# A decoder block: the third group's attention keys computed by seven products in the stage of the queries

## The chip, the cores and the metric

The kernel runs on one core of one Trainium2 chip. The time is the device time of one execution in microseconds; smaller is better. Five engines work beside each other, each with an instruction queue of its own that it takes in order: PE (TensorE, matrix products; PEld is its weight load), DVE (VectorE), ACT (ScalarE), POOL (GpSimd) and SP (SyncE, which here only starts transfers). Transfers (DMA) are issued from the queues of SP, POOL or ACT and run on 16 engines of their own. [...]

## The reference

For one sequence of 1024 tokens and width 1024, the block computes `h`, a normalized and modulated input, then one projection `h @ w_in` that is cut into parts, and from these a retention branch, an attention branch and gates; a squared-ReLU MLP follows. What matters here is the attention:

```
ATT_GROUPS = ((128, 1), (512, 4), (2048, 16))     # window, dilation; 4 heads of 128 each
for gi, (win, dil) in enumerate(ATT_GROUPS):
    aq, ak, av = parts[4 + 3 * gi], parts[5 + 3 * gi], parts[6 + 3 * gi]
    ...
    s = einsum(q, k) * dh ** -0.5 + bias           # banded, in blocks of 128 queries
    mx = max(s); e = exp(s - mx); den = sum(e); p = e / den; lse = mx + log(den)
    o = einsum(p, v)
wts = softmax(stack(lses), axis=0)                 # over the three groups
att = einsum('gbhs,gbhsd->bshd', wts, outs)
merged = sigmoid(gate_a) * ret_out + sigmoid(gate_b) * att_out
```

All is in float32.

## The kernel before

*Precision.* A float32 factor is split into a high part (`hi`, a cast) and a low part (`lo`, what is left), and a product is three matmuls: low by high, high by low, high by high (`mm3`, lines 207, 209, 211). The cast is made by ACT, the subtraction by DVE. So whatever PE is to multiply needs one instruction on each of the two first.

*Two ways to project.* Plain: `proj_gen` takes a head's weights (128 columns) and goes through the 1024 inputs in 8 k-steps; a k-step is 6 matmuls of 128x128 by 128x512 (two halves of the tokens, three terms), so a head takes 48. By seven products: the class `Blocks` takes a pair of heads (256 columns) as a 2 x 2 block problem and makes seven block products instead of eight, with sums of blocks before and after on DVE; each product is 12 matmuls, so a pair takes 84 where the plain way takes 96. The stage `queries_keys` runs 18 such pairs, in the order of the string `"rargrargrargrargaa"`: r are the queries and keys of the retention (each followed by a rotation on DVE, spread over the next pair), a the attention queries, g eight of the gates. Loads of a pair are issued when the pair two ahead of it starts. `a_out` evicts the results; attention queries are stored to DRAM (`aq_d`) and read again in the attention stage.

*The order around the change.* After the queries come the values, then the retention by heads and chunks, and then the attention, for two pairs of heads one after the other. The whole is a list of steps (`Steps`). A step has a body and a list of loads; each load is 512 KB into one of three buffers (`raw`), and has a function that splits it for PE. A buffer is loaded again as soon as its split is done. The splits of the next step's loads are emitted at the start of a step (`following`), or, for steps marked "late" or True, where the body calls for them. Nothing is scheduled by a planner: the engines' queues have the order in which the body emits.

*The attention of one pair of heads* has six key steps (`att_step`), in the order group 1, 2, 0 and within it head 0, 1. Step i projects one head's keys (8 k-steps) and weaves between the k-steps the scores of the step before (`scores_gen`, a "bank" being one PSUM bank of score blocks: three banks for group 1, two for group 2, four for group 0; `lag=2` means that the first bank comes after three k-steps). At its end it splits the new keys from PSUM (`k_split`, lines 1488 and 1489) and calls `scores_end` on the woven scores: maximum on DVE (lines 1529 to 1539), then eight exponentials on ACT (line 1542). After the second head of groups 1 and 2, `stats_out` stores maxima and sums to DRAM and reads them back in token order, both from SP. Then come gate steps (`cover_step`), which project gates so that PE has work: step 0 weaves the last scores, and emits `scores_end`, `weights` (the mix over groups), `pscale` (scaling of group 0's probabilities, lines 1645 and 1647), and the copy of the raw gate out of PSUM (lines 1827, 1828); step 1 is the gate alone; step 2 starts the products of probabilities and values (`pv`, each with a transpose, a split and its matmuls). The second pair's first key step lies beside the last of these products.

*Other work that lies there.* At the first key step the last head of the retention is finished (`u_final`: scale on ACT, product on DVE, store of `y` from SP, lines 687 to 690). Afterwards the sums of `y` blocks that the retention's output product wants are made by POOL's accumulating transfers, two at each projection (`with_sums`, `result_sum`, lines 572 and 574), each waiting for the one before. The bias tiles are loaded by SP at the end of the first key step (`bias_load`, line 1466).

Of the kernel before, what the change touches and what calls it, by code (L numbers as in the profile page):

```python
# [11 lines left out]
F32 = mybir.dt.float32  # L12
# [5 lines left out]
P = 128  # L18
D = 1024
S = 1024  # L20
# [120 lines left out]
def block_kernel(ctx, tc, io, stop=None, dbg=None):  # L141
# [537 lines left out]

    def u_final(h, es=range(4)):  # L680
        for e in es:
            i = h * 4 + e
            t = hd["on", h][e]
            for hf in range(2):
                neg = 16 if hf == i % 2 else 0
                b = t[:, 512 * hf:512 * hf + 512]
                nc.scalar.activation(b, b, AF.Identity, scale=gnv[0][:, neg + i:neg + i + 1],
                                     bias=gnv[1][:, neg + i:neg + i + 1])
            nc.vector.tensor_mul(t, t, hd["srg", h, e])
            nc.sync.dma_start(y_d[h][:, 2 * (i % 2):2 * (i % 2) + 2, e // 2], t.rearrange("p (t x) -> p t x", t=2))  # L690

# [78 lines left out]
    va_d = [dram.tile([S, 512], F32, name=f"vad{g}") for g in range(3)]  # L770
    aq_d = {(p, g, a): dram.tile([P, S], F32, name=f"aqd{p}{g}{a}") for p in range(2) for g in range(3) for a in range(2)}
    h12_d = [dram.tile([P, 2, 512], F32, name=f"h12d{m}") for m in range(4)]
    xn, wa = [], []
# [361 lines left out]
    g_pairs = [("g", i) for i in range(len(GATES) // 2)]  # L1135
    PAIRS = [{"r": r_pairs, "a": a_pairs, "g": g_pairs}[i].pop(0) for i in "rargrargrargrargaa"]
    NA = len(PAIRS)
    OA = {}

    def a_load(q, part):  # L1140
        pair = PAIRS[q]
        src = io[{"g": "w_gate2", "a": "w_aq"}.get(pair[0]) or f"w_r{pair[1]}"]
# [22 lines left out]
    def a_out(q, n, x, y=None):  # L1165
# [5 lines left out]
        o, view = OA[q][i][:, 512 * t:512 * t + 512], lambda z: z  # L1171
        if pair[0] == "a" and pair[1] == 1:
            o = OA[q][i].rearrange("p (r n i) -> p r n i", r=4, n=2)[:, :, t, :]
            view = lambda z: z.rearrange("p (i r) -> p r i", r=4)
        elif pair[0] == "a" and pair[1] == 2:
            o = OA[q][i].rearrange("p (r i) -> p r i", r=8)[:, :, 64 * t:64 * t + 64]
            view = lambda z: z.rearrange("p (i r) -> p r i", r=8)
# [7 lines left out]
        if n in ("12", "21"):  # L1185
            if pair[0] == "g":
                dst = gate_d[GATES[2 * pair[1] + i]]
            elif pair[0] == "a":
                dst = aq_d[pair[2], pair[1], i]
            else:  # L1190
                return
            nc.sync.dma_start(dst, OA[q][i])
# [282 lines left out]
    def q_prep(pair, g, a):  # L1475
# [6 lines left out]
        return prep  # L1482

    def k_split(pair, g, a, ps):

        hi, lo = ring(f"kh{pair}{g}{a}"), ring(f"kl{pair}{g}{a}")
        src, h_, l_ = by_blocks(ps, g), shaped(hi, g), shaped(lo, g)
        nc.scalar.copy(h_, src)
        nc.vector.tensor_sub(l_, src, fv(h_))
        A["k", g, a] = (hi, lo)  # L1490
# [34 lines left out]

    def scores_end(pair, g, a):
        p, t, st = A["p"], A["P", g, a], A["st"]
# [10 lines left out]
        ng = p.tile([P, 8], F32, tag="ng", bufs=2, name=f"ng{pair}{g}{a}")  # L1538
        nc.vector.tensor_scalar_mul(ng, st[:, g, :, a], -1.0)  # L1539
        for blk in range(8):  # L1540
            v = pslice(g, t, blk)[0]
# [58 lines left out]
    def stats_out(pair, g):  # L1600

        if g == 1:
            A["stn"] = A["p"].tile([P, 3, 8, 4], F32, tag="stn", name=f"stn{pair}")
        d = dram.tile([S, 4], F32, name=f"std{pair}{g}")
        nc.sync.dma_start(natural(d, g, 4), blocks(A["st"][:, g], g))
        nc.sync.dma_start(A["stn"][:, g], natural(d, 0, 4))

# [142 lines left out]

    combos = [(g, a) for g in (1, 2, 0) for a in range(2)]

    def att_step(pair, i):

        g, a = combos[i]

        def body(*args):
            ps = ps_mm(f"ak{pair}{i}")
            gen = with_sums(proj_gen(ps, args[-1]))
            if i == len(combos) - 2:  # L1760
                v_fetch(pair, 0)
            if i > 0:
                last = combos[i - 1]
                weave(gen, NK, scores_gen(pair, *last), len(SB[last[0]]), lag=2)
            elif pair == 0:
# [4 lines left out]
                drain(gen)  # L1770
                u_final(H - 1)
                for h in range(H):
# [3 lines left out]
            else:  # L1776

                gen = at(at(gen, 3, args[0]), NK - 1, lambda: k_split(pair, g, a, ps))
                weave_pv(gen, NK - 1, 0, 2)
            if i == 0:  # L1780
                A["st"] = A["p"].tile([P, 3, 8, 4], F32, tag="st", name=f"st{pair}")
                bias_load(pair)
            if i > 0 or pair == 0:
                k_split(pair, g, a, ps)
            if i > 0:
                scores_end(pair, *last)
                if last[1] == 1:
                    stats_out(pair, last[0])
        return body

    def cover_step(pair, n):
# [4 lines left out]
        def body(*args):  # L1796
            ps = ps_mm(f"gate0{i}")
            gen = with_sums(proj_gen(ps, args[-1]))
            if n == 0:
                v_fetch(pair, 1)  # L1800
                weave(gen, 6, scores_gen(pair, *combos[-1]), len(SB[0]), lag=2, rest=False)
                drain(gen)
                v_split(pair, 0, False)
                scores_end(pair, *combos[-1])
                weights(pair)
# [12 lines left out]
            else:  # L1818
                gen = at(at(gen, 3, lambda: [pscale(2, a) for a in range(2)]), 4, lambda: args[0](1))
                gen = at(at(at(gen, 6, lambda: v_split(pair, 2)), 6, args[0]), 6, sigmoids)  # L1820
                weave_pv(gen, NK - 1, pair, 1)
            if n > 1:
                t = A["r1"].tile([P, S], F32, tag="att", bufs=8, name=f"g0{i}s")
# [19 lines left out]
    for pair in range(2):  # L1843
        for i, (g, a) in enumerate(combos):
            steps.add(att_step(pair, i),
                      [wsplit(io["w_ak"][g * 4 + 2 * pair + a])] +
                      ([(aq_d[pair, *combos[i - 1]], q_prep(pair, *combos[i - 1]))] if i > 0 else []),
                      manual=("late" if pair else True) if i == 0 else False)
        for n in range(len(COVER[pair])):
            more = [(aq_d[pair, *combos[-1]], q_prep(pair, *combos[-1]))] if n == 0 else []  # L1850
            steps.add(cover_step(pair, n), more + [wsplit(io["w_gate"][len(COVER[0]) * pair + n])], manual={2: True, 3: "late"}.get(n, False))

# [898 lines left out]
def pack(x, c, w_ada, b_ada, norm1_g, w_in, rel_bias, ret_gn_g, ret_gn_b,  # L2751
# [18 lines left out]
        "w_aq": _pairs(att[:, :, 0].reshape(1024, 1536)),  # L2770
        "w_ak": _cols(att[:, :, 1].reshape(1024, 1536)),
        "w_av": _vcols(att[:, 0, 2], 512),
# [29 lines left out]
```

## Time and profile before

Three runs took 2181.95 to 2182.26 us, median 2182.03.

| | |
|---|---|
| profiled execution | 2182.64 us, span 2180.9 us |
| PE busy | 2156.0 us (99%), 10084 matmuls |
| DVE busy | 1491.7 us (68%) |
| ACT busy | 942.8 us (43%) |
| POOL busy | 164.0 us (8%) |
| granted clock of PE | 0.999 |
| moved by DMA | 416.78 MB, mean 191 GB/s |

Times in rows are microseconds from the span's start, durations of single instructions in the groups are in ns. L is a line of the kernel. A row of the timeline gives start, duration, engine, line, operation, output <- inputs, shape, count, and in brackets how long the engine was idle before it and which instruction ended that. A row of the chain of waits gives who waited for whom, the total, the number of times and the longest. Rows that follow each other closely and are alike are merged (x2). Matmuls are pipelined: PE starts the next before the last has ended, so their durations add up to more than the time that they take.

### The profile page before, as it was taken

To read this page: it belongs to the slowest core of one execution; us is meant where nothing else is said; L and a number is where in the kernel's file an instruction comes from. 1 tells how busy PE (TensorE), PEld (TensorE's weight loads), DVE (VectorE), ACT (ScalarE), POOL (GpSimd) and SP (SyncE) were. 2 spreads that over 40 slices of the span, in tenths; PEclk is the share of its full clock that TensorE was granted. 3 is DMA by queue.
4 is the path that set the end of the run, shared out by engine and by line. 5 is a ranking of instruction groups with operands and counts; after the bars stand their busy time and mean duration, and the time that the engine had idled before them with its cause. 6 is when DMAs were issued, how large, how long until landed. Compare 5 with 4: busy or idle time off the path is not lost. (4 is left out here: it accounts for less than half of the span.)

```text
span 2180.9 us, 27323 instructions
## 1 busy us (share of the span) xinstructions
PE 2156.0 (99%) x10084; PEld 1791.6 (82%) x10084; DVE 1491.7 (68%) x2333; ACT 942.8 (43%) x1729; POOL 164.0 (8%) x195
## 2 busy tenths in 40 slices
PE   8999999999999999999999999999999999999998
PEld 6888888888878888888888888888778888888887
DVE  5985777774467877854655644776876665877855
ACT  5553323323434544544644625434454545533413
POOL 0001111100012212211100000001000000000003
PEclk9999999999999999999999999999999999999999
DMA  9859998844685555557763275654254435645322
GB/s 383 289 209 297 296 298 257 243 119 174 237 301 170 198 174 194 181 172 190 184 167 108 81 268 189 224 186 139 65 182 150 153 136 194 249 137 175 111 87 78
DMA packets 160881, 416.78 MB, mean 191 GB/s; under 512 B 27749, under 2 KB 55660, under 8 KB 157676
## 3 DMA queue, kind: packets, MB, share of 16 engines
q1 hardware_dynamic: 151416, 368.67, 47.9%
q0 software_dynamic: 9008, 46.14, 9.9%
q8 instruction: 79, 1.29, 0.2%
q14 instruction: 54, 0.44, 0.1%
q10 hardware_dynamic: 324, 0.23, 0.0%
HBM read 319.93 MB, written 156.13 MB: 218 GB/s over the span
## 5 line engine op out<-in xcount | busy, mean ns | idle before, releaser
L207 PE MATMUL qap<-hh,qaw 128*128 128x512 f32 x216 | 84.0, 389 | 0.0
L209 PE MATMUL qap<-hl,qaw 128*128 128x512 f32 x216 | 84.0, 389 | 0.0
L211 PE MATMUL qap<-hh,qaw 128*128 128x512 f32 x216 | 84.0, 389 | 0.0
L617 POOL TENSOR_TENSOR j<-qk,j 128x512 fp32r<-128x512 f32 x32 | 43.2, 1351 | 412.4 <-ACT j L616 393.8
L2122 POOL TENSOR_TENSOR accnf<-accnf,sqnf 128x256 f32<-128x256 f32 (+1 forms) x18 | 16.6, 922 | 609.9 <-ACT sqnf L2118 609.9
L2226 ACT ACTIVATE a<-a 128x512 f32<-128x512 f32 x48 | 30.3, 631 | 73.7 <-DVE a L2225 73.7
L1542 ACT ACTIVATE P<-P,ng 128x128 f32<-128x128 f32 (+1 forms) x96 | 42.0, 439 | 36.6 <-DVE ng L1539 36.6
L2434 ACT CAST w2h<-w2s 128x512 fp32r<-128x512 f32 x36 | 22.4, 622 | 78.7 <-DVE w2s L2472 78.7
L264 DVE TENSOR_TENSOR fw<-w1r,fw 128x512 fp32r<-128x512 f32 x48 | 32.9, 688 | 33.6 <-ACT fw L254 33.6
L1957 DVE TENSOR_TENSOR rwl<-rwl,rwh 128x1024 fp32r<-128x1024 f32 x25 | 30.2, 1220 | 29.1 <-ACT rwh L1987 29.1
L207 PE MATMUL fp<-h2h,fw 128*128 128x512 f32 x128 | 50.0, 391 | 0.0
L211 PE MATMUL fp<-h2h,fw 128*128 128x512 f32 x128 | 49.8, 389 | 0.0
L209 PE MATMUL fp<-h2l,fw 128*128 128x512 f32 x128 | 49.8, 389 | 0.0
L207 PE MATMUL roa<-rh,rwl 128*128 128x512 f32 x128 | 49.8, 389 | 0.0
L209 PE MATMUL roa<-rl,rwh 128*128 128x512 f32 x128 | 49.8, 389 | 0.0
L211 PE MATMUL roa<-rh,rwh 128*128 128x512 f32 x128 | 49.8, 389 | 0.0
L652 ACT COPY sm<-sT 128x128 f32<-128x128 f32 x32 | 8.5, 266 | 93.7 <-PE sT L640 93.7
L207 PEld LDWEIGHTS qap<-hh,qaw 128*128 128x128 f32 x216 | 40.5, 188 | 8.5
L209 PEld LDWEIGHTS qap<-hl,qaw 128*128 128x128 f32 x216 | 40.5, 188 | 8.4
L211 PEld LDWEIGHTS qap<-hh,qaw 128*128 128x128 f32 x216 | 40.5, 188 | 8.4
L2122 POOL TENSOR_TENSOR accn<-accn,sqn 128x512 f32<-128x512 f32 x12 | 15.5, 1293 | 386.1 <-ACT sqn L2118 386.1
L1947 ACT ACTIVATE rh<-rl 128x512 fp32r<-128x512 f32 x56 | 31.7, 623 | 23.4 <-PE roc L209 8.4
(3097 smaller groups left out, 7251.4 us busy)
## 6 DMA issues: line engine op xcount, KB each, us to landing
v<-vd SPq DMA_DIRECT2D x32, 512.0 KB, 4.5
raw<-in_w_ada_dram SPq DMA_DIRECT2D x32, 512.0 KB, 5.3
w1r<-in_w_ff_dram SPq DMA_DIRECT2D x32, 512.0 KB, 4.6
yt<-y POOLq DMA_DIRECT2D x24, 512.0 KB, 7.6
xsd<-as SPq DMA_DIRECT2D x24, 512.0 KB, 2.8
w2r<-in_w_ff2s_dram SPq DMA_DIRECT2D x24, 512.0 KB, 6.9
em<-in_w_ada_dram SPq DMA_DIRECT2D x16, 512.0 KB, 10.2
wrvs<-in_w_rv_dram POOLq DMA_DIRECT2D x16, 512.0 KB, 10.0
```

What stands on the lines that cost most here:

```text
L207: nc.tensor.matmul(o, wl, xh, start=first, stop=False, skip_group_check=skip)
L209: nc.tensor.matmul(o, wh, xl, start=False, stop=False, skip_group_check=skip)
L211: nc.tensor.matmul(o, wh, xh, start=False, stop=last, skip_group_check=skip)
L264: nc.vector.tensor_sub(t[:, 512:], src, fv(t[:, :512]))
L617: nc.gpsimd.tensor_sub(t[:, 1], src, fv(t[:, 0]))
L652: nc.scalar.copy(sm, ps[:, :C])
L1542: nc.scalar.activation(v, v, AF.Exp, bias=ng[:, blk:blk + 1], accum_out=st[:, g, blk, 2 + a:3 + a])
L1947: nc.scalar.activation(hi, fv(lo), AF.Copy, scale=sign)
L1957: nc.vector.tensor_sub(lo, fv(lo), fv(hi))
L2122: (nc.vector if f == 7 else nc.gpsimd).tensor_add(G["acc", key], G["acc", key], sq)
L2226: nc.scalar.activation(o, o, AF.Relu)
L2434: nc.scalar.copy(hi, src)
```

## The change

- The four heads' keys of group 2 are no longer projected in the attention. Two pairs ("k") are added to the seven-product stage; the order there becomes `"rargrarkrargrarkgaga"`, 20 pairs. The keys are evicted as the queries of that group are, stored to DRAM (`ak_d`), and loaded in the attention as the queries are, with a split of their own (`k_prep`).
- The attention of a pair has four key projections. Those of group 1 stay as steps of their own (`att_step`). Each of group 0 is cut into two halves of four k-steps, which are two steps (`att_first`, `att_second`): the first half weaves the scores of group 1's second head, or group 2's second; the second half those of group 2's first head, or of group 0's first. The first bank comes after two k-steps (`lag=1`).
- Each half begins with `softmax`: read of stored statistics, maximum of the scores woven in the step before, then the splits of the next step's loads alone, then the exponentials and the store of the statistics. Before, maximum and exponentials stood together at the end of the step, ahead of the next step's splits, and the splits ran up to two steps ahead.
- Gate step 0 begins in the same way with group 0's first head. At its end the gate is copied out of PSUM by DVE in one piece, ahead of `weights`; before, it was copied by DVE and ACT in halves after `pscale`. The weights of gate step 2 are now split at the start of step 1.
- The store of the statistics is issued by ACT, the read by SP a step later. The last four stores of `y` are issued by POOL.
- POOL's sums are emitted at two projections fewer per pair of heads, and what is left follows at the last gate step.

```
-    PAIRS = [{"r": r_pairs, "a": a_pairs, "g": g_pairs}[i].pop(0) for i in "rargrargrargrargaa"]
+    k_pairs = [("k", 2, p) for p in range(2)]
+    PAIRS = [{"r": r_pairs, "a": a_pairs, "g": g_pairs, "k": k_pairs}[i].pop(0) for i in "rargrarkrargrarkgaga"]
...
-    def u_final(h, es=range(4)):
+    def u_final(h, es=range(4), queue=nc.sync):
...
-            nc.sync.dma_start(y_d[h][:, 2 * (i % 2):2 * (i % 2) + 2, e // 2], t.rearrange("p (t x) -> p t x", t=2))
+            queue.dma_start(y_d[h][:, 2 * (i % 2):2 * (i % 2) + 2, e // 2], t.rearrange("p (t x) -> p t x", t=2))
...
+    def k_prep(pair, a):
+        def prep(raw):
+            hi, lo = ring(f"kh{pair}2{a}"), ring(f"kl{pair}2{a}")
+            nc.scalar.copy(hi, raw)
+            nc.vector.tensor_sub(lo, raw, fv(hi))
+            A["k", 2, a] = (hi, lo)
+        return prep
...
-        d = dram.tile([S, 4], F32, name=f"std{pair}{g}")
-        nc.sync.dma_start(natural(d, g, 4), blocks(A["st"][:, g], g))
-        nc.sync.dma_start(A["stn"][:, g], natural(d, 0, 4))
+        d = A["std", g] = dram.tile([S, 4], F32, name=f"std{pair}{g}")
+        nc.scalar.dma_start(natural(d, g, 4), blocks(A["st"][:, g], g))
+
+    def stats_in():
+        for g in (1, 2):
+            if ("std", g) in A:
+                nc.sync.dma_start(A["stn"][:, g], natural(A.pop(("std", g)), 0, 4))
...
+    def softmax(splits):
+        stats_in()
+        if scored:
+            scores_max(*scored[0])
+        splits(1)
+        if scored:
+            pair, g, a = scored.pop()
+            scores_exp(pair, g, a)
+            if g > 0 and a == 1:
+                stats_out(pair, g)
...
+    HALF = NK // 2
+    def att_first(pair, a):
+        def body(*args):
+            A["kp"] = ps_mm(f"ak{pair}0{a}")
+            A["kg"] = with_sums(proj_gen(A["kp"], args[-1]))
+            done = (1, 1) if a == 0 else (2, 1)
+            softmax(args[0])
+            if a == 1:
+                v_fetch(pair, 0)
+            weave(itertools.islice(A["kg"], HALF), HALF, scores_gen(pair, *done), len(SB[done[0]]), lag=1)
+            scored.append((pair, *done))
+        return body
+    def att_second(pair, a):
+        def body(*args):
+            done = (2, 0) if a == 0 else (0, 0)
+            softmax(args[0])
+            weave(A["kg"], HALF, scores_gen(pair, *done), len(SB[done[0]]), lag=1)
+            k_split(pair, 0, a, A["kp"])
+            scored.append((pair, *done))
+        return body
...
             if n == 0:
                 v_fetch(pair, 1)
-                weave(gen, 6, scores_gen(pair, *combos[-1]), len(SB[0]), lag=2, rest=False)
+                softmax(args[0])
+                weave(gen, 6, scores_gen(pair, 0, 1), len(SB[0]), lag=2, rest=False)
                 drain(gen)
                 v_split(pair, 0, False)
-                scores_end(pair, *combos[-1])
+                scores_max(pair, 0, 1)
+                scores_exp(pair, 0, 1)
+                t = ring(f"g0{i}s", F32)
+                nc.vector.tensor_copy(t, flat(ps))
+                raw_gates.append((i, t))
                 weights(pair)
...
+        steps.add(att_step(pair, 0), [w_load(1, 0)], manual="late" if pair else True)
+        steps.add(att_step(pair, 1), [w_load(1, 1), q_load(1, 0)])
+        steps.add(att_first(pair, 0), [w_load(0, 0), q_load(1, 1)], manual="late")
+        steps.add(att_second(pair, 0), [q_load(2, 0), k_load(0)], manual="late")
+        steps.add(att_first(pair, 1), [w_load(0, 1), q_load(2, 1), k_load(1)], manual="late")
+        steps.add(att_second(pair, 1), [q_load(0, 0)], manual="late")
```

More of the change, by code (lines that the diff above doesn't have):

```diff
@@ L771, in block_kernel @@
     aq_d = {(p, g, a): dram.tile([P, S], F32, name=f"aqd{p}{g}{a}") for p in range(2) for g in range(3) for a in range(2)}
+    ak_d = {(p, a): dram.tile([P, S], F32, name=f"akd{p}{a}") for p in range(2) for a in range(2)}
     h12_d = [dram.tile([P, 2, 512], F32, name=f"h12d{m}") for m in range(4)]
@@ L1189, in a_out @@
                 dst = aq_d[pair[2], pair[1], i]
+            elif pair[0] == "k":
+                dst = ak_d[pair[2], i]
             else:
@@ L1749, in weave_pv, with att_step @@
         drain(main)
-    combos = [(g, a) for g in (1, 2, 0) for a in range(2)]
-    def att_step(pair, i):
-        g, a = combos[i]
+    scored = []
+    def softmax(splits):
[8 more added lines that the diff above has]
+                stats_out(pair, g)
+    def att_step(pair, a):
         def body(*args):
-            ps = ps_mm(f"ak{pair}{i}")
+            ps = ps_mm(f"ak{pair}1{a}")
             gen = with_sums(proj_gen(ps, args[-1]))
[L1760 to L1764, printed above, removed]
+            if a == 1:
+                weave(gen, NK, scores_gen(pair, 1, 0), len(SB[1]), lag=2)
             elif pair == 0:
```

48 lines of the change are left out of this document (27 added, 21 removed).

## The prediction

> **What bounds the kernel now.** I read the page first, then the chain of waits of PE, then busy time by window, then the order of time of single steps.
>
> ```profile
> span 2180.9 us, 27323 instructions
> ...
> PE 2156.0 (99%) x10084; PEld 1791.6 (82%) x10084; DVE 1491.7 (68%) x2333; ACT 942.8 (43%) x1729; POOL 164.0 (8%) x195
> ```
>
> ```profile
> PE sc L209 <- DVE kl L1489: 0.4, 1, 0.4
> ...
> PE pv L1687 <- DVE ptl000(0, 0, 0)_9051 L1667: 0.3, 1, 0.3
> PE pv L1687 <- DVE ptl100(0, 0, 0)_10418 L1667: 0.3, 1, 0.3
> ```
>
> ```profile
> 180.10:523.00 342.90, 342.90 (x1514) 283.94 (x1513) 245.29 (x382) 100.01 (x174) 36.31 (x50) 1.00 0.79 238
> 955.50:969.84 14.34, 13.98 (x74) 11.76 (x73) 8.28 (x8) 5.92 (x7) 1.33 (x2) 1.00 1.00 287
> 944.00:1024.60 80.60, 80.24 (x414) 68.11 (x413) 40.76 (x48) 39.72 (x96) 9.47 (x14) 1.00 0.72 199
> ```
>
> The columns of the last fence are length, then PE, PEld, DVE, ACT and POOL busy, granted clock, DMA share, GB/s. PE is the bound: the stage of the queries (180 to 523 us) has no idle PE at all, the first pair's key steps (944 to 1025 us) 0.36 us of it, and the granted clock is 1.00. In both, DVE and ACT are far from full. The three waits shown are all that the changed steps leave idle. So the time moves by what PE no longer issues, less what its new order makes it wait for. Matmul durations overlap; the price of one is the distance of two starts:
>
> ```profile
> 180.12 0.39 PE L207 MATMUL qap<-hh,qaw 128*128 128x512 f32 x1
> ...
> 522.84 0.39 PE L207 MATMUL vc<-vwh,xat 128*128 128x512 f32 x1
> ```
>
> The stage between holds 18 pairs of 84 matmuls: 342.72 / 1512 = 0.2267 us each, not the 0.39 of the row.
>
> **The change part by part.**
>
> *Seven products.* A key head of the third group takes 8 k-steps of 6 matmuls, 48; four heads take 192, and go. Two "k" pairs take 7 products of 12 matmuls each, 168, and come. Net 24 fewer, by 0.2267: **-5.44 us**. Beside it each pair brings what every pair brings: 13.6 us of DVE (245.29/18) under 19.05 of PE, and ACT's 5.6. PE did not wait once in that stage, and r pairs, which carry the rotation on DVE, still alternate with others, so I cost it at nothing. Without that cover each of 14 products could lose up to DVE's excess; a PE wait on qap of 0.3 us each would be 4 us. The four writes and four reads of 512 KB through DRAM are queued on SP between loads that are issued two pairs ahead.
>
> *Shorter cover in the attention.* Per pair of heads the four key projections of 10.9 us under which group 2 ran are gone for two of them; scores and softmax are now laid under halves of group 0's projections. How long are the halves?
>
> ```profile
> 969.84 0.62 PE L207 MATMUL ak<-hh,raw_8107l 128*128 128x512 f32 x2
> ...
> 973.94 0.28 PE L207 MATMUL sc<-kh,ql 128*128 128x256 f32 x1
> ...
> 974.65 0.63 PE L207 MATMUL ak<-hh,raw_8107l 128*128 128x512 f32 x2
> ...
> 980.86 0.22 PE L207 MATMUL sc<-kh,ql 128*128 128x128 f32 x1
> ...
> 982.15 0.69 PE L207 MATMUL ak<-hh,raw_8107l 128*128 128x512 f32 x2
> ```
>
> Three k-steps take 4.10 us, a bank of 256-wide scores 0.71, one of 128-wide 1.29. First half of head 0: 4 x 1.37 + 2 x 0.71 + 1.29 = 8.2 us; second half and the next first half, with two banks of group 2: 8.05 each; the last, with four banks of group 0 (0.7 each): 8.3. The other engines need, by the step at 984:
>
> ```profile
> 983.85 1.01 ACT L1488 CAST kh<-ak 128x1024 fp32r<-128x1024 f32 x1 [3.85 <-PE ak L211]
> 988.08 0.40 ACT L1542 ACTIVATE P<-P,ng 128x128 f32<-128x128 f32 x1 [3.22 <-DVE ng L1539]
> ...
> 991.61 1.04 ACT L1479 ACTIVATE qh<-raw 128x1024 fp32r<-128x1024 f32 x1
> 992.56 1.03 ACT L197 CAST raw_8378h<-raw 128x1024 fp32r<-128x1024 f32 x1
> ```
>
> ```profile
> 984.90 1.23 DVE L1489 TENSOR_TENSOR kl<-ak,kh 128x1024 fp32r<-128x1024 f32 x1 [1.65 <-ACT kh L1488]
> 986.04 0.68 DVE L1534 TENSOR_REDUCE st<-P 128x4 f32<-128x512 f32 x1
> ...
> 987.88 0.17 DVE L1539 TENSOR_SCALAR ng<-st 128x8 f32<-128x8 f32 x1
> ```
>
> Eight exponentials take 991.61 - 988.08 = 3.53 us, a split about 0.95 on ACT and 1.14 on DVE (984.90 to 986.04), a maximum 1.9. The fullest half is the second of head 0: weights, query and key splits, exponentials and the store of the statistics, 2.9 + 3.5 + 0.6 = 7.0 us of ACT in 8.05, and on DVE 1.9 + 3.4 + 1.3 = 6.6. It fits, and neither order of maximum, splits and exponentials is late for PE: what a half's scores read was split a half earlier, so with the splits ahead of the exponentials PE waits for nothing. I cost this at 0.
>
> The store of the statistics now stands on ACT's queue ahead of the next key split; its price there is that of SP's issue:
>
> ```profile
> 991.73 0.62 SPq L1605 DMA_DIRECT2D std<-st  x1
> ```
>
> The split behind it is not read for another half (8 us), so 0.6 us are hidden. The read back, a step later on SP, no longer holds the loads behind it.
>
> *First bank one k-step sooner.* Scores started after three k-steps, now after two: 1.37 us less cover for the key split before it. In pair 0 that split ended late, because the adds ahead of it waited for the bias:
>
> ```profile
> 969.51 1.89 DVE L1519 TENSOR_TENSOR P<-sc,bias 128x512 f32<-128x512 f32 x3 [0.78 <-DMA bias<-biasd]
> 971.31 1.21 DVE L1489 TENSOR_TENSOR kl<-ak,kh 128x1024 fp32r<-128x1024 f32 x1
> ```
>
> ```profile
> 953.68 4.58 SPq L690 DMA_DIRECT2D y<-on  x4
> ...
> 961.22 3.27 SPq L1466 DMA_DIRECT2D bias<-biasd  x6
> ```
>
> It is ready at 972.52; PE, which ends the step at 969.84, would want it at 969.84 + 2.73 + 0.11 = 972.68. The margin is 0.16 us, so the wait lies between 0 and about 1.4. Moving the four stores of y to POOL takes 4.58 us off SP ahead of the bias, but the DMA engines were full there (share 1.00, 955 to 970 us) and the stores remain. [...] I take **+0.35**, the size of the one wait of this kind (960.20's, first line of the waits), once; in pair 1 the adds wait for no bias.
> On POOL the stores (nearest row: 0.88 us an issue) stand ahead of the chain of sums, which starts some 15 us later and has four sums left for the gate step; nothing reads them before the output products, 100 us on.
>
> ```profile
> 947.85 0.88 POOL L572 DMA_DIRECT2D yt<-y  x1 [4.33 <-DMA yt<-y]
> ```
>
> *Gate step 0 to gate step 2.* Here a part moves that could cost.
>
> ```profile
> 1035.83 0.67 PE L207 MATMUL gate<-hh,raw_8498l 128*128 128x512 f32 x2
> ...
> 1038.64 0.62 PE L207 MATMUL gate<-hh,raw_8599l 128*128 128x512 f32 x2
> ...
> 1049.88 0.72 PE L207 MATMUL gate<-hh,raw_8707l 128*128 128x512 f32 x2
> ```
>
> ```profile
> 1034.60 1.23 DVE L198 TENSOR_TENSOR raw_8707l<-raw,raw_8707h 128x1024 fp32r<-128x1024 f32 x1 [4.96 <-ACT raw_8707h L197]
> ...
> 1037.54 0.61 DVE L1523 TENSOR_TENSOR P<-sc,bias 128x256 f32<-128x256 f32 x2
> ...
> 1038.39 2.01 DVE L1530 TENSOR_REDUCE st<-P 128x7 f32<-128x1792 f32 x1
> ...
> 1046.02 2.58 DVE L1645 TENSOR_SCALAR P<-P,wt 128x128 f32<-128x128 f32 x10
> 1048.52 0.68 DVE L1827 COPY g00s<-gate 128x512 f32<-128x512 f32 x1
> ```
>
> ```profile
> 1040.64 0.40 ACT L1542 ACTIVATE P<-P,ng 128x128 f32<-128x128 f32 x1 [4.17 <-DVE ng L1539]
> ```
>
> Before, the weights of gate step 2 (raw_8707) were split within step 0, and DVE sat 4.96 us behind that, so the last score adds came late (1037.54), and with the maximum behind them the exponentials began 2.0 us after PE's end of the step (1038.64). In the new order step 0 splits only the weights of step 1, ahead of the exponentials; the adds follow PE, whose last bank is done by 1036.1, 1.4 us before DVE came to it, and the exponentials can begin about 1039.3. The gate's copy (2 x 0.68 less a start-up, 1.25) fits under them; the scaling ends about 1047.5 instead of 1048.6. But now the weights of step 2 are split behind the scaling: ACT 0.95 and DVE 1.2, ready at 1049.7. PE asks at 1049.88. So the bound is 0 if the sooner start comes true and 0.95 us if it does not. I take 0, as DVE's stall is plain in its row. The two copies of gate 0 that stood between scaling and the first products are gone, and with them the wait of 0.34 before the first pv of each pair: **-0.68** for two.
>
> Sum: -5.44 + 0.35 - 0.68 = -5.8 us. The profiled execution took 2182.64 us (span 2180.9 and 1.7 around it), 0.6 above the median of 2182.03; 5.8 off gives 2176.9 for it and **2176.2** for the median.
>
> **The rivals.**
>
> *Weights late.* Gate step 2's weights come 0.95 us late in both pairs and the pv waits stay, the bias wait grows to 1: -5.44 + 1.9 + 1 = -2.5, 2179.5. For it speaks a margin of 0.2 us; against it the 4.96 us row.
>
> *Loads late, slower.* Each pair's half-steps need the same loads in 22 us less, through three buffers. The second key's load is issued when the first key is split, 6.8 us into the first half; with landing time L and 2.2 us of splitting it is ready at 9.0 + L, and PE wants it at 8.2 + 8.05 + 2.73 = 19.0. The row for such loads:
>
> ```profile
> raw<-aqd SPq DMA_DIRECT2D x12, 512.0 KB, 6.3
> ...
> wa<-in_w_rk_dram SPq DMA_DIRECT2D x8, 512.0 KB, 12.5
> ```
>
> At 6.3 there are 3.7 us to spare; the wait is L - 10 a pair, and the first gate weights, two landings deep in the same buffers, add L - 11.4. At 12.5, the worst row for reads of this size in the queries' stage, 2 x (2.5 + 1.1) = 7.2 us, and with the sum 2183.4; from L = 12.2 the gain is gone, from 13.3 it is slower by 0.2%. Behind a late load ACT also holds the exponentials and the next key split, which this leaves out, so where it comes true I put most of it beyond 0.2%. Against it: the DMA share of 0.72, which the shorter steps raise to about 0.82.
>
> *Nothing saved.* The added pairs make PE wait as much in the queries' stage as their 24 matmuls save: about 2181. Against it, 343 us without an idle PE.
>
> **How the numbers follow.** About 0.2%, 4.4 us, is what a measurement of this kernel can tell from no change; the forecast is only 1.4 us beyond it. Forecast (2175.2 to 2177.6): 0.63, all faster. Weights late: 0.15, within 0.2%. Loads late: 0.19, of which 0.05 within 0.2% and 0.14 slower. Nothing saved: 0.03, within. So 0.63, 0.23, 0.14. The range reaches from the forecast with no wait at all (2175.2) up to 2181.5, which takes in weights late and the mild end of loads late; about 0.19 is left out.
>
> **What would show it.** In the changed profile: qap matmuls longer by 168 starts, still without idle PE; ak with 128 instead of 192 per term. PE's waits should list no pv at the first ptl of a pair, at most a small sc at kl in pair 0, and no gate weights at step 2. If raw loads from akd show landings above 10 us, or PE waits on kl of the copied keys, the loads were the step that failed; a wait on gate weights above 0.5 us means that the start of the exponentials did not move.

## The result, and the profile after

The changed kernel takes 2176.70 us (median of 12 runs, 2175.69 to 2179.79) against 2182.08 for the kernel before (12 runs, 2181.53 to 2183.95): a ratio of 0.9975, 95% interval 0.9967 to 0.9984. The profiled execution took 2179.79 us, the slowest of the twelve, so its trace may show waits that the median run does not have.

From the page of the changed kernel:

```profile
PE 2151.7 (99%) x10060; PEld 1789.6 (82%) x10060; DVE 1512.8 (69%) x2361; ACT 947.4 (43%) x1741; POOL 167.2 (8%) x199
...
L207 PE MATMUL qap<-hh,qaw 128*128 128x512 f32 x240 | 93.4, 389 | 0.0
```

24 matmuls fewer in all, and no idle time before any of the 240 products of this form (the last number). PE's waits in the changed kernel, total, times and longest:

```profile
PE kv L207 <- DVE kl L666: 3.1, 2, 2.5
PE rg L207 <- DVE vr L1322: 0.8, 1, 0.8
...
PE sc L209 <- DVE kl L1502: 0.4, 1, 0.4
```

The two pv waits at the first ptl of a pair are gone, the sc wait of 0.4 is the old one (first key step), and nothing in the attention waits for weights or copied keys. New are the first two rows, and they are not in the attention: kv and rg are the first products of the retention, a stage that the change does not touch.

Busy time by stage: queries, values, retention, attention. First the kernel before, then the changed one (columns as in the prediction; the clock is the third number from the end):

```profile
180.12:533.70 353.58, 353.58 (x1561) 292.79 (x1560) 248.86 (x385) 104.28 (x181) 36.31 (x50) 1.00 0.79 241
533.70:631.64 97.94, 97.94 (x434) 81.08 (x432) 48.68 (x62) 42.23 (x62) 7.12 (x10) 1.00 0.67 239
631.64:944.10 312.46, 310.44 (x1509) 257.27 (x1508) 244.89 (x514) 143.96 (x361) 58.44 (x63) 1.00 0.56 186
944.10:1250.70 306.60, 305.25 (x1693) 262.18 (x1692) 178.51 (x278) 168.25 (x372) 20.99 (x31) 1.00 0.57 156
```

```profile
180.50:572.20 391.70, 391.70 (x1729) 324.33 (x1729) 272.30 (x417) 114.79 (x200) 36.23 (x50) 1.00 0.73 228
572.20:671.10 98.90, 98.12 (x434) 80.91 (x432) 49.36 (x62) 41.77 (x61) 7.13 (x10) 1.00 0.68 240
671.10:986.87 315.77, 312.18 (x1509) 258.74 (x1509) 244.32 (x513) 143.69 (x361) 57.83 (x62) 0.99 0.54 183
986.87:1247.90 261.03, 260.32 (x1502) 226.19 (x1501) 175.68 (x274) 162.93 (x366) 24.87 (x36) 1.00 0.65 184
```

The queries grow by 38.12 us, the attention shrinks by 45.57: -7.45. (The stage before the queries ends 0.38 us later, 180.50 against 180.12; the profiled execution as a whole is 2.85 us shorter.) But values and retention, the same work on PE (434 and 1509 matmuls in both), are 0.96 and 3.31 us longer. In the retention PE is idle 3.59 us instead of 2.02, and busy 1.74 longer with the same matmuls. Let us see why, in the changed kernel's order of time (SP, ACT, PE), and then in windows of 1 us:

```profile
664.81 8.00 SPq L1326 DMA_DIRECT2D vd<-vr  x4
...
679.18 0.27 ACT L652 COPY sm<-sT 128x128 f32<-128x128 f32 x1 [7.45 <-DMA vd<-vr]
...
681.37 0.50 PE L207 MATMUL kv<-v,kl 128*128 128x512 f32 x1 [2.50 <-DVE kl L666]
```

```profile
681.00:682.00 1.00, 0.63 (x3) 0.53 (x4) 0.32 (x1) 0.00 (x0) 0.00 (x0) 0.96 1.02 362
682.00:683.00 1.00, 1.00 (x4) 0.81 (x3) 0.00 (x0) 0.00 (x0) 0.00 (x0) 0.50 1.13 358
683.00:684.00 1.00, 1.00 (x6) 0.81 (x4) 0.00 (x0) 0.00 (x0) 0.00 (x0) 0.50 1.02 367
684.00:685.00 1.00, 1.00 (x7) 1.00 (x6) 0.06 (x1) 0.27 (x1) 0.00 (x0) 0.50 1.14 351
685.00:686.00 1.00, 1.00 (x6) 0.78 (x5) 0.60 (x3) 0.41 (x2) 0.00 (x0) 0.83 0.86 324
```

ACT's first copy of the retention, into the tile sm, waits 7.45 us for a store of values (vr to vd) to land. kl (the low part of the retention's keys) is made behind it, and PE idles 2.50 us. Then the granted clock is 0.50 for three windows and a part of two more: 2 x (0.04 + 3 x 0.50 + 0.17) = 3.4 us at half speed, which costs the 1.7 us of longer busy time.

Why should sm wait for a store? The tiles of the retention take the memory of the tiles of the stages before (`open_ret` closes one pool and opens the next). In the memory map of the built program (a trace shows no addresses) of the kernel before, sm lies where a block of values stored early (vo71) lay. The two added pairs allocate more tiles from that pool, so that its blocks come in another order: in the changed kernel sm lies where vr11 lay, one of the last four stored. The same shift in PSUM gave rg the bank of the last vc block, which DVE had not yet read out. So the theory is: placement, not the work of the change. It forecasts an effect in both directions, and the first experiments test it.

### The profile page after: what moved, and what is told of

Read it like the earlier page. It is cut to its first block, busy times and chain, and to the rows that moved or that the text cites. A ratio compares the mean times of both kernels' runs of the same rounds, so it can differ in the third digit from the quotient of the medians.

```text
span 2178.0 us, 27354 instructions
## 1 busy us (share of the span) xinstructions
PE 2151.7 (99%) x10060; PEld 1789.6 (82%) x10060; DVE 1512.8 (69%) x2361; ACT 947.4 (43%) x1741; POOL 167.2 (8%) x199
## 5 line engine op out<-in xcount | busy, mean ns | idle before, releaser
L207 PE MATMUL qap<-hh,qaw 128*128 128x512 f32 x240 | 93.4, 389 | 0.0
L209 PE MATMUL qap<-hl,qaw 128*128 128x512 f32 x240 | 93.4, 389 | 0.0
L211 PE MATMUL qap<-hh,qaw 128*128 128x512 f32 x240 | 93.4, 389 | 0.0
L209 PEld LDWEIGHTS qap<-hl,qaw 128*128 128x128 f32 x240 | 45.0, 188 | 9.4
L211 PEld LDWEIGHTS qap<-hh,qaw 128*128 128x128 f32 x240 | 45.0, 188 | 9.3
L207 PEld LDWEIGHTS qap<-hh,qaw 128*128 128x128 f32 x240 | 45.0, 188 | 9.3
L264 DVE TENSOR_TENSOR qaw<-wa,qaw 128x512 fp32r<-128x512 f32 x60 | 40.0, 686 | 8.8 <-ACT qaw L254 8.8
L292 DVE TENSOR_TENSOR qat<-qat,qap 128x512 f32<-128x512 f32 x20 | 13.7, 687 | 46.4 <-PE qap L211 46.4
```

What stands on the lines that cost most here:

```text
L207: nc.tensor.matmul(o, wl, xh, start=first, stop=False, skip_group_check=skip)
L209: nc.tensor.matmul(o, wh, xl, start=False, stop=False, skip_group_check=skip)
L211: nc.tensor.matmul(o, wh, xh, start=False, stop=last, skip_group_check=skip)
L264: nc.vector.tensor_sub(t[:, 512:], src, fv(t[:, :512]))
L292: nc.vector.tensor_sub(u, u, b)
```

## The experiments

**Moving the tiles.** One line moves: `chunk_tiles`, which allocates sm, kl and their like, comes behind the state tiles. By the memory map this puts them on long finished blocks in the changed kernel; in the kernel before the same line puts a part of kl on vr13, the block stored last.

```
         open_ret()
-        chunk_tiles()
...
         R["state"] = R["p"].tile([P, 2, DV], F32, name="state")
+        chunk_tiles()
```

In the changed kernel:

> The changed kernel with one line moved: the retention's first small tiles (the call of chunk_tiles) are allocated behind its state tiles. Nothing else of the program changes. Theory (placement): in the changed kernel PE idles 2.5 us before its first kv product, since the copy into sm, the first tile of the retention, waits for the store of a vr block that lay in the same place, and 3.4 us at half clock follow. With sm where a long finished tile lay, that wait and the half clock go; PE's wait of 0.8 us at rg stays. The retention stage (first rg to first ak) takes 312.5 us as in the kernel before instead of 315.8. By stages 2182.0 + 38.1 (queries) - 45.6 (attention) + 1.0 (rg) = 2175.5, between 2175.1 and 2175.9, and the runs lie within 1 us of each other. Rival (the transfers at the end of the values are late whatever waits for them, and another instruction will wait): 2176.7, with a spread of 4 us as in the changed kernel.

Measured: 2176.10 us (10 runs, nine within 2175.02 to 2176.62, one at 2180.42; before beside it 2182.69). The time itself lies between the two forecasts, but the kernel before was 0.7 us slower beside this run than the 2182.0 that they start from. Against it the gain is 6.59 us, where the theory's time gives 6.5 and the rival's 5.3. The trace says the same. Its window from rg to the first key step:

```profile
671.40:983.30 311.90, 310.63 (x1509) 257.48 (x1510) 244.37 (x513) 143.71 (x361) 57.80 (x62) 1.00 0.55 185
```

311.9 us, as in the kernel before; the wait of 2.5 and the half clock are gone, rg's 0.8 remains. The one late run stays unexplained. Each kernel has one traced execution, so it is not shown that this store is what spread the changed kernel's twelve runs.

In the kernel before:

> The kernel before with the same line moved as in the first run. There the move does the opposite: the tile kl of the first chunk comes to lie partly where the last vr block lay, whose store is issued last, at 634.3 us, and lands some 9 us later. Theory (placement): kl is written at about 643.5 instead of 636.4 us, PE's first kv product starts at about 644 instead of 639.1, 4.8 us late, and half a window of clock (1.7 us) is lost after it; part is won back by later waits of 1 us: 2187, between 2185 and 2189. Rival (the wait belongs to the two added pairs and not to the place): no change, 2182.0.

Measured: 2187.13 us (11 runs, 2186.50 to 2188.52), ratio to before 1.0020 (1.0011 to 1.0029): the same line that helps there costs 4.4 us here. Its DVE and PE, and its retention window:

```profile
642.39 0.48 DVE L666 SCALAR_TENSOR_TENSOR kl<-kT,ct,kh 128x256 fp32r<-128x256 f32 x1 [5.87 <-DMA vd<-vr]
...
642.93 0.80 PE L207 MATMUL kv<-v,kl 128*128 128x512 f32 x1 [3.65 <-DVE kl L666]
```

```profile
631.60:948.70 317.10, 312.17 (x1510) 258.30 (x1509) 245.06 (x514) 143.70 (x361) 58.42 (x63) 0.99 0.55 184
```

4.64 us longer than the 312.46 before, of which 1.73 is busy time, again one stretch at half clock (3.4 us, by the granted clock in two windows from 639 to 646.6 us). Placement is shown as the cause, both ways, on a kernel with and one without the change.

**Moving the PSUM banks too.** With the line moved, a score bank is also allocated before the first rg, so that rg gets other banks:

```
             hd["rgw"] = w
+            if g == 0:
+                ps_s("first")
             hd["rgp"] = ps_mm(f"rg{h}{c}")
```

> As the run before, and the retention's PSUM banks are shifted: a score bank is allocated ahead of the first gate projection, so that rg takes two banks whose last users, vc and va blocks, were evicted earlier, and not the bank of the last vc block. Theory (placement): the 0.8 us that PE waits at rg for DVE's eviction of the last vc block vanish too, with about 0.2 of restart: 2174.5, between 2174.1 and 2174.9. Rival (PE needs that eviction anyway, for instance because the next product waits for ACT or DVE at the same point): 2175.5, like the run before.

Measured: 2175.04 us (5 runs, 2174.64 to 2175.98), ratio to before 0.9966 (0.9953 to 0.9978). The time is above the theory's range, but against the kernel before beside it (2182.69) the gain is 7.65 us, where the theory's time gives 7.5 against 2182.0 and the rival's 6.5. The changed kernel gained 5.38 against the kernel before beside it (2182.08), so the two moves together are worth 2.3 us. The stages of values, retention and attention:

```profile
571.70:669.60 97.90, 97.90 (x433) 81.07 (x432) 48.79 (x62) 42.32 (x62) 7.13 (x10) 1.00 0.68 239
669.60:981.60 312.00, 310.42 (x1509) 257.27 (x1508) 245.05 (x514) 143.79 (x361) 57.77 (x62) 1.00 0.56 187
981.60:1242.60 261.00, 260.32 (x1501) 226.18 (x1501) 175.89 (x274) 162.90 (x366) 24.60 (x36) 1.00 0.66 184
```

Both waits are gone and the attention is what it was. All further runs start from this kernel. Its five runs lie within 1.3 us and those of the kernels made from it within 0.7 to 4.4, so differences of some tenths are read from the traces, not from the medians.

**The order of maximum, splits and exponentials.** My prediction had it that either order has room. First the exponentials ahead of the splits:

```
             scores_max(*scored[0])
-        splits(1)
-        if scored:
             pair, g, a = scored.pop()
             scores_exp(pair, g, a)
             if g > 0 and a == 1:
                 stats_out(pair, g)
+        splits(1)
```

> The second run's kernel (moved tiles and banks, 2175.0 us, attention stage 261.0 us) with the splits of the next step's loads behind the exponentials and the store of the statistics, instead of between maximum and exponentials; nothing is left out. Theory (the place between matters in one step): in the second half of head 0 of group 0 the exponentials then start at about 23.75 us where the splits did, take 3.5, the store 0.6, and the weights of the next half are ready at 30.2 where PE asks for them at 29.1 (counted in the changed kernel's trace from 1000 us): a wait of 1.1 us and 0.3 of restart in each pair, and up to 0.2 at gate step 0's weights: +2.5 over the second run, between +1.5 and +3.5. Rival (either order has room, as my prediction says of both orders, neither late for PE): +0 to +0.5.

Measured: 2201.52 us (4 runs, 2201.24 to 2201.95), 26.5 over its base, ten times my figure. Its waits, and its attention stage:

```profile
PE ak L207 <- DVE raw_9791l L198: 4.9, 1, 4.9
PE gate L207 <- DVE raw_8733l L198: 4.0, 1, 4.0
PE gate L207 <- DVE raw_9991l L198: 3.0, 1, 3.0
PE ak L207 <- DVE raw_8533l L198: 2.0, 1, 2.0
```

```profile
982.30:1269.60 287.30, 271.18 (x1501) 232.66 (x1500) 174.52 (x274) 162.86 (x366) 24.72 (x36) 0.96 0.61 167
```

The wait that I had worked out is there, 2.0 us at the weights raw_8533. What I had not followed is how it goes on, in the next half (DVE and ACT):

```profile
1041.43 1.23 DVE L1486 SCALAR_TENSOR_TENSOR ql<-raw,qh 128x1024 fp32r<-128x1024 f32 x1 [4.21 <-ACT qh L1485]
...
1045.35 0.40 ACT L1563 ACTIVATE P<-P,ng 128x128 f32<-128x128 f32 x1 [3.95 <-DVE ng L1555]
```

The high part of q stands behind one half's exponentials on ACT; DVE waits 4.21 us for it, and the next maximum stands behind that low part on DVE; so ACT's next exponentials wait 3.95 us, and the gate's weights, split behind them from 1050.00, are 4 us late for PE. Each engine in turn holds the other. Pair 1 loses 4.9 and 3.0. Idle time grows by 15.4 us (287.30 - 271.18 = 16.1 against 0.7), and busy time by 10.9 at a granted clock of 0.96; in pair 0 two stretches at half clock, of 6.8 and 3.4 us by windows, lie in this stage.

Then the other way round, the splits ahead of both:

```
+        splits(1)
         if scored:
             scores_max(*scored[0])
-        splits(1)
-        if scored:
             pair, g, a = scored.pop()
```

> The second run's kernel with the splits of the next step's loads ahead of maximum and exponentials both; the other half of the question that the run with the exponentials first asked (it took 26 us more, with PE waiting 2 to 5 us for weights and 20.5 us at half clock). Theory formed after that run (what counts is that the weights of the next half and the loads behind them do not stand behind the exponentials; where the maximum stands matters little): the maximum's 1.9 us and the exponentials come up to 3.5 us later, the next key split on ACT with them, and PE reads nothing of that before two more k-steps: +0 to +1 over the second run, no wait of PE on weights, no half clock. Rival (the maximum behind the splits makes the exponentials and then the next splits late in a chain, as before): +5 or more.

Measured: 2182.23 us (11 runs, 2180.54 to 2184.90; before beside it 2183.20): +7.2 in medians, 6.7 when each is taken against the kernel before beside it. Nearly the whole gain is lost, and my second theory fell as well. The waits of its profile:

```profile
PE sc L207 <- ACT kh L1503: 2.8, 2, 1.6
PE sc L209 <- DVE kl L1504: 2.1, 3, 0.9
```

Here the exponentials start late, since the maximum stands behind the low parts on DVE, and the split of the projected key, queued behind them on ACT, comes after PE asks for it, in both pairs. The gate's weights are late by 0.7 and 0.4 us besides. The waits are short (1.6 at most), and the granted clock of this stage is 1.00. So both places matter: of the three orders only the one with the maximum ahead of the splits and the exponentials behind them leaves PE without these waits.

**The first bank and the issuer of y.** The last four stores of y on SP again, then, in a second run, y on POOL and the first bank after three k-steps (here in `att_second`, alike in `att_first`):

```
-                u_final(H - 1, queue=nc.gpsimd)
+                u_final(H - 1)
```

> The second run's kernel with the last four stores of y issued by SP again, ahead of the bias. In the changed kernel the adds of the first scores start 12.5 us after the end of the first key step, in the kernel before 14.0, and the key split behind the adds is ready 0.4 us before PE reads it. Theory (the issuer decides when the bias lands): the bias comes 1.5 us later, and PE waits for the key split about 1.2 us, once: +1.2 over the second run, between +0.8 and +2. [...] My prediction's own term for this place was +0.35 with POOL's issue; the changed kernel's trace shows no such wait.

```
-            weave(A["kg"], HALF, scores_gen(pair, *done), len(SB[done[0]]), lag=1)
+            weave(A["kg"], HALF, scores_gen(pair, *done), len(SB[done[0]]), lag=2)
```

> The second run's kernel with the first bank of scores after three k-steps of each half, not two (as in the steps before the change). My prediction gave the sooner bank +0.35, one wait of PE for the first key split of pair 0; the changed kernel's trace shows none, but a margin of 0.4 us, and with y issued by SP the wait was 0.25. Theory (the sooner bank costs nothing while the margin holds): -0.1 to +0.3. Rival (the later bank delays the last adds, the maximum and the splits behind them by 1.4 us, and PE waits for the weights of the next half): +1 to +4.

Measured: 2175.62 (5 runs, 2174.74 to 2176.60) and 2175.51 (5 runs, 2174.12 to 2176.15), neither to be told from 2175.04. With y on SP the rows of SP, DVE and PE are:

```profile
991.40 5.80 SPq L690 DMA_DIRECT2D y<-on  x4
998.16 3.29 SPq L1472 DMA_DIRECT2D bias<-biasd  x6
...
1007.59 1.89 DVE L1534 TENSOR_TENSOR P<-sc,bias 128x512 f32<-128x512 f32 x3 [7.45 <-DMA bias<-biasd]
...
1010.28 0.28 PE L207 MATMUL sc<-kh,ql 128*128 128x256 f32 x1
1010.66 0.39 PE L209 MATMUL sc<-kl,qh 128*128 128x256 f32 x1
```

with y on POOL, those of SP and DVE:

```profile
996.97 3.51 SPq L1472 DMA_DIRECT2D bias<-biasd  x6
...
1005.45 1.89 DVE L1534 TENSOR_TENSOR P<-sc,bias 128x512 f32<-128x512 f32 x3 [5.53 <-DMA bias<-biasd]
```

The stages begin 0.2 us apart (981.85 and 981.64), so with y on POOL the bias lands 1.9 us sooner. On SP the key split is late and PE loses 0.25 us (starts 0.38 apart instead of the usual 0.12); on POOL nothing. I had expected 1.2, but with POOL DVE had 1.26 us to spare between adds and key split, waiting for ACT, and the delay eats that first.

The row of 5.80 us is not what four issues cost. Rows that are alike are merged, waits included. A single store of y takes SP 0.38 us to issue, and the four follow DVE's products, 1.41 us apart, for which POOL has to wait as well (first SP with y on SP, then POOL with y on POOL):

```profile
948.02 0.38 SPq L690 DMA_DIRECT2D y<-on  x1
```

```profile
993.02 0.73 POOL L690 DMA_DIRECT2D y<-on  x1 [0.62 <-DVE on L689]
```

So the move brings the bias's first issue 1.0 us forward (998.16 - 996.97, less the 0.2). The other 0.9 us come behind the issue: the bias loads of 128 KB take 7.4 us to land instead of 8.5 (medians). POOL's sums also lie at other times in the two runs; what made the loads land faster was not tried.

**The gate step.** Weights of gate step 2 two steps ahead, as before the change:

```
-                softmax(args[0])
+                softmax(lambda n: args[0](2))
```

> The second run's kernel with the weights of gate step 2 split within gate step 0, two steps ahead as in the kernel before. My prediction's theory: DVE then sits behind the landing of those weights (4.96 us in the kernel before), the last score adds and the last exponentials of the pair begin 1.35 us later, scaling and first products come late, and the two pv waits return, 0.34 us each and as much again for PE's restart: +1.4, between +0.7 and +2. Rival (by the changed kernel's trace these weights land some 5 us before the last add, so that only the exponentials of head 0 move, and they have room): +0, between -0.2 and +0.3.

Measured: 2175.37 us (6 runs, 2174.35 to 2177.57), attention 260.9 us, no new wait: the rival's time. ACT has those weights when they land, and DVE, which first has the maximum to do, does not stand still for them:

```profile
1044.54 1.05 ACT L197 CAST raw_8877h<-raw 128x1024 fp32r<-128x1024 f32 x1 [2.56 <-DMA raw<-in_w_gate_dram]
```

The raw gate copied behind the scaling, in halves, as before the change:

```
-                t = ring(f"g0{i}s", F32)
-                nc.vector.tensor_copy(t, flat(ps))
-                raw_gates.append((i, t))
                 weights(pair)
...
-            if n == 0:
-                return
```

> The second run's kernel with the raw gate of step 0 copied as in the kernel before: by DVE and ACT in halves, after the scaling. Theory (the copy between scaling and first products made the pv waits): 0.6 us on ACT and DVE ahead of the split of gate step 2's weights, which are ready 0.64 us before PE asks; they and the first split of probabilities come 0.6 us later: the pv wait of 0.34 returns in each pair, with restart 0.7: +1.4, between +0.7 and +1.6. Rival, from the margins of the changed kernel's trace (0.64 us at the weights, 0.9 at the first ptl): +0 to +0.3.

Measured: 2175.78 us (6 runs, 2175.42 to 2177.26), +0.7 in medians (the two sets of runs overlap), and in the profile the attention is 262.3 us, +1.3. The pv waits do not return; another takes their place:

```profile
PE gate L207 <- DVE raw_8877l L198: 0.5, 1, 0.5
PE gate L207 <- DVE raw_10136l L198: 0.4, 1, 0.4
```

The copies hold the split of gate step 2's weights back by more than the 0.64 us that it was ahead of PE.

**Late keys.** In the changed kernel the second copied key of pair 0 is loaded from 1019.27 us, and ACT takes it when it lands:

```profile
1024.96 1.06 ACT L1492 CAST kh<-raw 128x1024 fp32r<-128x1024 f32 x1 [0.78 <-DMA raw<-akd]
```

Six copies go ahead of that load on SP, and of its like in pair 1:

```
+                for d in getattr(flat[i][1], "copies", ()):
+                    nc.sync.dma_start(d, flat[i][0])
                 raw = self.pool.tile([P, 1024], F32, tag="raw", name=f"raw{i}")
...
+        if a == 1:
+            prep.copies = [dram.tile([P, S], F32, name=f"copy{pair}{i}") for i in range(6)]
```

> The second run's kernel with six copies of 512 KB from DRAM to DRAM issued by SP ahead of each load of a second copied key of group 2 (one per pair of heads): they only make it late. Theory (the rival of my prediction, loads late: wait = L - 10 a pair, where L is the time from the moment the load could be issued to its landing, now 5.6 us; the trace of the changed kernel agrees, the key is split 4.5 us before PE reads it): six copies take 8 to 10 us, L is 14 to 16, PE waits 4 to 6 us for kl of the copied key in each pair, with 1.7 us of half clock behind it, and the loads behind it add some: +8 to +17 over the second run, 2183 to 2192. Rival (that load is not near the path): +0 to +1.

Measured: 2198.16 us (4 runs, 2195.82 to 2200.25), +23.1. The copies took longer than I had worked out; from the first copy's issue to the key's landing it is 20.3 us in pair 0 and 16.8 in pair 1. PE's waits for the two keys:

```profile
PE sc L209 <- ACT kh L1496: 12.4, 2, 8.0
PE sc L211 <- DVE kl L1497: 1.6, 2, 0.8
```

That is 8.8 us in pair 0 and 5.3 in pair 1, where L - 10 gives 10.3 and 6.8: the formula is right to 1.5 us, with a limit at 11.5. The attention stage took 284.9 us, 23.9 more, for 14.0 us of waits; nearly all the rest, 9.8, is longer busy time, at a granted clock of 0.95: behind each of the two waits for a key the scores on PE start 0.21 us apart, where 0.11 is usual, and its rows stay that slow from 1036.2 to 1042.6 us in pair 0 and from 1175.6 to 1185.5 in pair 1.

## Why the prediction was right, point by point

The median of 2176.7 is 0.5 us over the forecast of 2176.2. But errors on the two sides stand against each other, so that the number comes this close is partly luck: the attention gained more than my terms, and stages that I had left out lost time. (The lower end of my range, 2175.2, is named there as the forecast with no wait; the terms give 2182.03 - 5.44 - 0.68 = 2175.9.)

- *Seven products, -5.44.* Right. The queries grew by 38.12 us, worked out 168 x 0.2267 = 38.09, with no idle PE; the cover of DVE and ACT was enough, as costed.
- *Shorter cover, 0.* The outcome was right, the sentence "neither order of maximum, splits and exponentials is late for PE" was wrong. I added up ACT and DVE over a half step (7.0 and 6.6 of 8.05 us) and found that it fits. The sum leaves out one split: the three in it are those of the loads, and that of the head's own keys at the end of the same half is a fourth. In the run with moved tiles and banks ACT makes the three from 1016.65 us, and the fourth here:

```profile
1024.06 1.01 ACT L1503 CAST kh<-ak 128x1024 fp32r<-128x1024 f32 x1 [0.84 <-PE ak L211]
```

With 0.95 us more on ACT and 1.14 on DVE the half is full: 7.95 and 7.74 of 8.05. And order within the half counts as much as the sum: what stands behind the exponentials is late and passes the delay to the other engine (4.21 us to DVE and 3.95 back to ACT with the exponentials first). The two other orders cost 7 and 26 us. The order that the change has is the only one of the three in which the change gains time.

- *First bank, +0.35.* Mis-sized: no run shows this term; the wait is 0 in the changed kernel, 0.25 with y on SP. The 4.58 us that I took off SP's queue were a misreading of the kind shown above: four issues of about 0.38 us, spread by DVE's products. And I had taken the move to POOL to bring the bias little sooner, which was my estimate, from the DMA share of 1.00 there. With y on POOL it landed 1.9 us sooner than with y on SP: 1.0 of that is its sooner issue; the other 0.9 are not time of issue, and the runs leave open what brought them.
- *Gate step, -0.68.* Right in sign, too small in size, and its cause not borne out. The two pv waits went. But each had cost more than its listed 0.34: in the kernel before the two starts around one are 0.73 us apart, where 0.12 is usual. What removed them stays open. I had made DVE's stall behind the weights of two steps ahead the reason; split early again in the new order, those weights cost nothing, but the stall did not come back with them, so its part is not tested. The copy ahead of `weights` is worth 1.3 us of the attention, but put back it makes the gate's weights late and not the products of probabilities. The exponentials start 0.50 us behind PE's end of the step, where I had 0.65, and the weights of step 2 are ready 0.64 us ahead, where I had 0.2:

```profile
1059.01 0.62 PE L211 MATMUL gate<-hh,raw_8721h 128*128 128x512 f32 x2
...
1059.96 0.40 ACT L1561 ACTIVATE P<-P,ng 128x128 f32<-128x128 f32 x1 [4.28 <-DVE ng L1553]
1068.83 1.23 DVE L198 TENSOR_TENSOR raw_8876l<-raw,raw_8876h 128x1024 fp32r<-128x1024 f32 x1 [0.91 <-ACT raw_8876h L197]
1070.70 0.70 PE L207 MATMUL gate<-hh,raw_8876l 128*128 128x512 f32 x2
```

- *Loads late.* As a rival it did not come true (L is 5.6 us for pair 0's second copied key), but the mechanism and its limit are real (waits of 8.8 and 5.3 us in the run with late keys, a limit of 11.5), and the landing of 12.5 us that I had quoted as the worst would have made it bite.
- *What I did not see.* The attention gained 45.57 us where my terms give 43.53 - 0.35 + 0.68 = 43.9: 1.7 more (by the distance of starts, ak gave 44.2 and pv 1.4). And values and retention lost 4.3 in the profiled execution: rg's 0.96, which the profile of the run with moved tiles alone shows too, and the rest mostly by the wait for a store's landing and the half clock behind it. No step of mine looked at a stage without changed code; the two pairs' tiles moved the places of later tiles in memory, and with them what these wait for.

## What to carry to other kernels

Work added in one stage shifts which memory a later stage's first tiles reuse, and so which store or read-out they wait for: after such a change compare the stages that were not changed, at their first instructions. Where two engines are nearly full in a step and feed each other, follow their queues in order instead of summing the step, and count every split that the step makes. Before you read a merged row as the cost of its instructions, look for the waits inside it. Price an idle PE at more than the wait that is listed: 0.2 to 0.3 us of restart here (0.73 - 0.12 - 0.34 = 0.27 at the first pv wait of the kernel before), and behind some waits half clock (3.4 us of it behind the 2.50 in the changed kernel). In the two runs that had most of it, wait and half clock together cost 1.7 times the idle time.

## What the runs showed of the hardware

I had not expected the half clock inside a busy kernel. In the changed kernel PE idles 2.50 us, starts again at 681.37, and 0.6 us later runs at half speed for 3.4 us. With the exponentials first one stretch is 6.8 us long, from 1022.9 (by windows of 2 us), and with late keys PE's rows are slow for 6.4 and 9.9 us. In the run with the exponentials first only two waits, of 0.52 and 0.74 us within 1.6 us, stand shortly ahead of the 6.8 us (PE; then a window of busy time at half clock), and the wait of 1.95 us at 1031.34 was not followed by any (granted clock 1.00 from 1031 to 1036 us):

```profile
1019.75 0.30 PE L207 MATMUL sc<-kh,ql 128*128 128x128 f32 x1 [0.52 <-DVE ql L1486]
1020.79 0.33 PE L209 MATMUL sc<-kl,qh 128*128 128x128 f32 x1 [0.74 <-DVE kl L1495]
```

```profile
1023.00:1029.00 6.00, 6.00 (x21) 4.98 (x20) 1.55 (x3) 3.63 (x17) 1.64 (x3) 0.50 0.64 183
```

So the length of one wait does not tell whether half clock follows; what else decides it was not tried. In sum, 15.4 us of added idle time came with 10.9 us of longer busy time in that run, and 14.0 with 9.8 with late keys.
